# Router scale vectors stored in rows, router weight product behind the first output tile, routing in the order of the first gather

## The chip, the cores and the metric

The kernel runs on one core of a Trainium2 chip as one program. The metric is the device time of one execution in microseconds, the median of three timed runs. Beside them stands one profiled execution of the same program, from which every row below is taken.

## The reference, cut to what matters

The model takes one sequence of 512 tokens of width 1024 in f32. Four first layers (two short convolutions, a state space mixer, an RWKV mixer) are followed by two layers that each hold a token mixer and a hierarchical mixture of 32 experts. The change touches the step from the second kind of token mixer into its mixture of experts, in both layers:

```python
for l in range(DEPTH_2):
    mod = (c_act @ w_ada[l] + b_ada[l])[:, None, :]
    sh1, sc1, g1, sh2, sc2, g2 = jnp.split(mod, 6, axis=-1)
    h = rms_norm(x, norm1_g[l]) * (1 + sc1) + sh1
    x = x + g1 * token_mixer(h, ...)
    h = rms_norm(x, norm2_g[l]) * (1 + sc2) + sh2
    x = x + g2 * hierarchical_moe(h, router_group_w[l], router_group_b[l],
                                  router_expert_w[l], router_expert_b[l], w1[l], w3[l], w2[l])
```

The mixture picks for each token the best of 4 groups of experts and in it the two best of 8 experts, weighs them by a softmax, and adds the two experts' outputs (`silu(h @ w1) * (h @ w3)) @ w2`, with expert matrices of 1024x512, 1024x512 and 512x1024).

## The kernel before, in words

A tile scheduler lays the instructions of each engine in one order when the program is built; `self.behind(ins)` is a hint to it that what is issued inside stands behind the instruction `ins`. On the chip every engine then works through its list in that order, so an instruction that waits holds up all that stand behind it on its engine. SP issues the DMAs, also in order.

**The end of a token mixer.** `moe_before` (L2198) prepares the router while the mixer still runs. For the first of the two layers it stores four vectors of 1024 numbers, the gains `gs` and the shifts `mod` of both layers, into a DRAM scratch `d_gp` (L2205, L2206). In SBUF such a vector lies as 128 partitions by 8 columns, in DRAM as 8 rows of 128, so the store goes element by element. L2477 reads them back as `gp` in the layout that the gather of the experts needs. Then come the loads of the router's weights `wr` and bias `rb` (L2209, L2210), the product `gw` of weights and gains on VectorE (L2211), eight matmuls of `wr` with the shifts (L2214), and their sum with `rb` (L2215). The mixer's last matrix `w_out` is loaded in eight parts through the helper at L338, split into two halves of the f32 precision on ScalarE and VectorE (L315, L317), and multiplied at L423; `out_sink` adds each of the eight result tiles into the residual `xp`. In the second half of the tiles `moe_part` (L2222) also forms the router's logits from `gw`.

**Routing.** `route` is a generator in three parts. The first part (to L2302) finds group and experts of each token, forms the softmax weights `wts` (L2274 to L2281), ranks each token in its expert (`cs`, `rk`, `rx`, `r8`), and computes on GpSimd the slots `main0` of the tokens of the two static experts 0 and 1 (L2295 to L2302). The second part ranks all experts by their counts (`key`, `big`, `rank`, `ecap`, `nb`, L2306 on) and yields the list `eii` of experts in order of size. `moe_gather` (L2444) turns slots into selection matrices: GpSimd writes `Ra` and VectorE `R` for four blocks of tokens (L2454, L2455), and matmuls of `R` with the two halves of the hidden state (L2464) give the gathered tokens, which ScalarE scales into `xg` (L2468).

**The experts.** Expert weights come in loads of 1 MB (L2394) into 11 buffers, `raw`; an expert takes six (two of `w1`, two of `w3`, two of `w2`). Experts 0 and 1 are static, so 11 of their 12 loads are issued before routing is done. All others are loaded by the number read from `eii`. `moe_up` (L2401) multiplies by `w1` and `w3` (L2411), `moe_down` (L2423) by `w2` (L2438). Between routing and the first expert stands `overflow` (L2659, L2663), a loop for tokens beyond an expert's slots whose count is read from `eii`; its head and its end are points at which all engines wait for each other. In the profiled execution the loop has no pass.

```python
first = self.moe_gather(l, main, *GROUPS[0], gx)
next(first)
main = next(route)
self.fill(first, 99)
wts, over, eii = next(route)
...
    self.overflow(l, eii, over, wts)
...
    gs = self.moe_up(ws, gx[g], units)
```

## Time and profile before

| | |
|---|---|
| median of 3 timed runs | 3358.76 us (3357.37 to 3361.43) |
| profiled execution | 3351.78 us |
| its span, first to last instruction | 3350.0 us |
| granted TensorE clock, mean over the span | 0.921 |
| first four layers, then the modulation and mixer of layer 0 | 0 to about 1934 us |
| mixture of experts of layer 0 | about 1934 to 2490 us |
| mixer of layer 1 | about 2490 to 2790 us |
| mixture of experts of layer 1 | about 2790 to 3350 us |

The profile gives for each engine when it worked and, where it stood idle, what ended the idle time. PE is TensorE, DVE VectorE, ACT ScalarE, POOL GpSimd, SP the engine that issues the DMAs. A granted clock of 1.00 is TensorE's level of 2.4 GHz, 0.50 that of 1.2 GHz.

### The profile page before, as it was taken

The page shows a single profiled execution, that of the slowest core. Times are in us where ns is not written, and L with a number is a line of the kernel's source. Part 1 is how long each engine was busy: PE and PEld are TensorE (multiplying, and loading weights), DVE is VectorE, ACT ScalarE, POOL GpSimd, SP SyncE. Part 2 cuts the span into 40 slices and gives each one's busy share as a digit, 9 for nine tenths or more (in the row PEclk, how much of TensorE's full clock was granted, in tenths as well). Part 3 has the DMA queues.
Part 4 walks back from the last instruction along what each step waited for, and adds up shares of the span by engine and source line. Part 5 has one row for each costly group of instructions (what it writes and reads, how often), then busy time and mean ns, then how long its engine had stood idle before and what let it go on. Part 6 is the DMA issues. An engine that isn't in the chain of part 4 may idle for free. (4 is left out here: it accounts for less than half of the span.)

```text
span 3350.0 us, 57495 instructions
## 1 busy us (share of the span) xinstructions
PE 2979.4 (89%) x23218; PEld 2154.2 (64%) x23218; DVE 2016.2 (60%) x3911; ACT 1032.3 (31%) x1696; POOL 882.7 (26%) x738
## 2 busy tenths in 40 slices
PE   7999889988889898999789979989979996998997
PEld 5677768865557777777655756555647565655554
DVE  6754495467875778798847554534436845354443
ACT  3233324356533433222343421111125342111111
POOL 2911331125422456421205220100111423010000
PEclk9999899989889898999788979999989887999999
DMA  5453463314679545676340049999972003899998
GB/s 170 135 157 101 127 165 102 104 63 127 176 212 251 166 150 176 195 219 205 104 53 20 26 189 360 408 409 416 415 272 70 28 20 152 307 415 410 416 416 337
DMA packets 443070, 690.46 MB, mean 206 GB/s; under 512 B 68720, under 2 KB 354800, under 8 KB 408944
## 3 DMA queue, kind: packets, MB, share of 16 engines
q1 hardware_dynamic: 441648, 684.63, 58.9%
q8 instruction: 185, 3.03, 0.4%
q10 hardware_dynamic: 1152, 2.10, 0.2%
q14 instruction: 85, 0.70, 0.1%
HBM read 642.08 MB, written 46.94 MB: 206 GB/s over the span
## 5 line engine op out<-in xcount | busy, mean ns | idle before, releaser
L317 DVE TENSOR_TENSOR wl<-wr,wh 128x1024 fp32r<-128x1024 f32 (+2 forms) x275 | 327.8, 1194 | 213.6 <-ACT wh L315 110.4
L315 ACT ACTIVATE wh<-wr 128x1024 fp32r<-128x1024 f32 (+2 forms) x290 | 271.0, 939 | 532.6 <-PE pmm L423 177.6
L2411 PE MATMUL pmm<-raw,xg 128*32 128x128 f32 (+1 forms) x5120 | 351.4, 324 | 2.7 <-DMA raw<-in_w_dram 2.5
L2411 PEld LDWEIGHTS pmm<-raw,xg 128*32 128x32 f32 (+1 forms) x5120 | 228.2, 123 | 121.0 <-issue 48.8
L2558 POOL TENSOR_SCALAR Ra<-sp,cf 128x512 f32<-128x512 f32 x28 | 44.6, 1593 | 795.0 <-PE pst L2597 744.3
L423 PE MATMUL pmm<-H,wh 128*128 128x512 f32 x680 | 205.7, 412 | 12.2 <-ACT wh L315 8.2
L423 PE MATMUL pmm<-L,wh 128*128 128x512 f32 x680 | 203.1, 406 | 3.7 <-DVE L L317 2.2
L423 PE MATMUL pmm<-H,wl 128*128 128x512 f32 x680 | 202.3, 405 | 1.5 <-DVE wl L317 1.5
L2573 DVE SCALAR_TENSOR_TENSOR xp<-pst,mod,xp 128x512 f32<-128x512 f32 x196 | 143.0, 748 | 64.8 <-PE pst L2598 60.5
L2438 PE MATMUL pas<-raw,gT 128*32 128x256 f32 (+1 forms) x1472 | 171.1, 465 | 12.0 <-DVE gT L2432 9.8
L423 PEld LDWEIGHTS pmm<-H,wh 128*128 128x128 f32 x680 | 130.6, 197 | 45.0 <-ACT wh L315 9.9
L1561 DVE SCALAR_TENSOR_TENSOR war<-wa,cs,war 128x256 f32<-128x256 f32 x252 | 157.1, 640 | 3.5
L423 PEld LDWEIGHTS pmm<-L,wh 128*128 128x128 f32 x680 | 130.7, 194 | 37.0 <-DVE L L317 4.1
L423 PEld LDWEIGHTS pmm<-H,wl 128*128 128x128 f32 x680 | 131.4, 195 | 33.7 <-DVE wl L317 2.4
L2648 ACT COPY Y<-pas 32x256 f32<-32x256 f32 (+1 forms) x92 | 37.8, 411 | 298.9 <-DVE Y L2648 298.8
L2464 PE MATMUL pst<-R,hH 128*128 128x320 f32 (+4 forms) x448 | 92.7, 323 | 33.4 <-DVE R L2455 30.8
L2438 PEld LDWEIGHTS pas<-raw,gT 128*32 128x32 f32 (+1 forms) x1472 | 61.2, 122 | 93.8 <-issue 61.0
L2648 DVE COPY Y<-pas 32x256 f32<-32x256 f32 (+1 forms) x92 | 43.7, 475 | 128.7 <-PE pas L2438 120.2
L2418 DVE TENSOR_TENSOR g<-g,pmm 128x256 f32<-128x256 f32 (+1 forms) x56 | 20.3, 363 | 162.3 <-ACT g L2417 162.0
L2417 ACT ACTIVATE g<-pmm 128x256 f32<-128x256 f32 (+1 forms) x56 | 18.9, 338 | 294.0 <-PE pmm L2411 294.0
L2411 PE MATMUL pas<-raw,xg 128*32 128x128 f32 (+1 forms) x2048 | 97.8, 292 | 10.9 <-SPq L2518 6.8
L2464 PEld LDWEIGHTS pst<-R,hH 128*128 128x128 f32 x448 | 69.7, 202 | 56.7 <-DVE R L2455 35.6
(869 smaller groups left out, 6729.2 us busy)
## 6 DMA issues: line engine op xcount, KB each, us to landing
raw<-in_w_dram SPq DMA_DIRECT2D x384, 1024.0 KB, 12.4
wa<-in_w_ada_dram SPq DMA_DIRECT2D x48, 1024.0 KB, 5.9
wr<-in_conv_w_in_dram SPq DMA_DIRECT2D x64, 512.0 KB, 4.7
wr<-in_w_in_dram SPq DMA_DIRECT2D x34, 512.0 KB, 4.1
wr<-in_ple_gate_dram SPq DMA_DIRECT2D x16, 1024.0 KB, 5.5
wr<-in_rwkv_w_rkvz_dram SPq DMA_DIRECT2D x16, 1024.0 KB, 5.7
wr<-in_conv_w_out_dram SPq DMA_DIRECT2D x8, 1024.0 KB, 5.2
wr<-in_ssm_w_in_dram SPq DMA_DIRECT2D x8, 1024.0 KB, 6.5
```

What stands on the lines that cost most here:

```text
L315: self.nc.scalar.activation(h, x, AF.Copy)
L317: (eng or self.nc.vector).tensor_tensor(l, x, h.bitcast(FT), OP.subtract)
L423: nc.tensor.matmul(ps[i], ws[i][w][:, perm[k]], x[k], start=n == first[i], stop=n == last[i])
L1561: E.scalar_tensor_tensor(acc, w[:, k], cs[:, k:k + 1], acc, op0=OP.mult, op1=OP.add)
L2411: nc.tensor.matmul(p[c * n:c * n + n, w // 2 * W:w // 2 * W + W], x[:, j, o:o + n], ws[w][:, jj, c * W:c * W + W], start=j == 0, stop=j == 7)
L2417: nc.scalar.activation(g, p[:, 0:W], AF.Sigmoid)
L2418: nc.vector.tensor_tensor(g, g, p[:, 0:W], OP.mult)
L2438: nc.tensor.matmul(py[q * n:q * n + n, 0:W], gT[:, o:o + n], ws[4 + j // 2][:, j % 2, q * W:q * W + W], start=j == 0, stop=j == 3)
L2464: T.matmul(p[:, :n], (self.hH, self.hL)[i // 4][:, i % 4, j], R[:, i % 4, :n], start=i == 0, stop=i == 7)
L2558: G.tensor_scalar(a, P[0], s, None, op0=OP.is_equal)
L2573: self.done = self.nc.vector.scalar_tensor_tensor(self.xp[m], p, self.mod[l][:, 40 + m:41 + m], self.xp[m], op0=OP.mult, op1=OP.add).ins
L2648: (nc.scalar.copy if q % 2 else nc.vector.tensor_copy)(self.block[1][o:o + n, q * W:q * W + W], p[q * n:q * n + n])
```

## The change

Four things change; all other code stays.

1. `moe_before` no longer stores the four vectors element by element. PE transposes each into 8 rows of 128, ScalarE copies the 8x512 tile to SBUF, and one DMA stores its rows into `d_gp`.
2. The product `gw`, the eight matmuls with `wr` and the sum with `rb` move into `moe_weights`, which is issued behind the first output tile (`first_sink`, m = 0). The loads of `wr` and `rb` stay where they were.
3. In `route`, `main0` is computed on VectorE in five instructions instead of on GpSimd in eight; the copy `sh` of the slots falls away where its offset is 0; the softmax weights are formed behind `main0`; and the second part is issued behind the last `R` of the first gather.
4. In `moe`, `moe_up` of the experts 0 and 1 and the twelfth load of the static experts are issued ahead of `overflow`.

```diff
--- before.py
+++ after.py
@@ -2179,12 +2179,18 @@
 
 
         def out_sink(m, p):
-            V.scalar_tensor_tensor(self.xp[m], p, self.mod[l][:, 16 + m:17 + m], self.xp[m], op0=OP.mult, op1=OP.add)
+            return V.scalar_tensor_tensor(self.xp[m], p, self.mod[l][:, 16 + m:17 + m], self.xp[m], op0=OP.mult, op1=OP.add).ins
+
+        def first_sink(m, p):
+            done = out_sink(m, p)
+            if m == 0:
+                with self.behind(done):
+                    self.moe_weights(l)
 
         def last_sink(m, p):
             out_sink(m, p)
             self.moe_part(l, m)
-        for h, sink in enumerate((out_sink, last_sink)):
+        for h, sink in enumerate((first_sink, last_sink)):
             o = order[h * 4:h * 4 + 4]
             self.dense(([z["H", k] for k in o], [z["L", k] for k in o]), A["w_out"][l][h * 512:h * 512 + 512], range(0, D, 256),
                        sink, kt=4, perm=[k - h * 4 for k in o])
@@ -2201,17 +2207,26 @@
         if self.d_gp is None:
 
             self.d_gp = d = self.dr.tile([2, 2, 8, 128], FT, name="d_gp")
+            p = self.pt("tp", bufs=2)
             for i in range(2):
-                nc.sync.dma_start(d[i, 0].rearrange("k p -> p k"), self.gs[i][:, 8:16])
-                nc.sync.dma_start(d[i, 1].rearrange("k p -> p k"), self.mod[i][:, 24:32])
-        wr, self.gw, self.rb = (self.c2.tile([128] + sh, FT, name=f"{n}{l}", tag=n, bufs=1)
-                                for n, sh in (("wr", [8, 36]), ("gw", [8, 36]), ("rb", [36])))
-        nc.sync.dma_start(wr, self.A["w_router"][l].rearrange("(k p) n -> p k n", p=128))
+                for j, t in enumerate((self.gs[i][:, 8:16], self.mod[i][:, 24:32])):
+                    o = (2 * i + j) * 128
+                    nc.tensor.transpose(p[0:8, o:o + 128], t, self.ident)
+            t = self.wt("rows")
+            nc.scalar.activation(t[0:8], p[0:8], AF.Copy)
+            nc.sync.dma_start(d.rearrange("i j k p -> k (i j) p"), t[0:8].rearrange("k (n p) -> k n p", n=4))
+        self.wr, self.gw, self.rb = (self.c2.tile([128] + sh, FT, name=f"{n}{l}", tag=n, bufs=1)
+                                     for n, sh in (("wr", [8, 36]), ("gw", [8, 36]), ("rb", [36])))
+        nc.sync.dma_start(self.wr, self.A["w_router"][l].rearrange("(k p) n -> p k n", p=128))
         nc.sync.dma_start(self.rb, self.A["rb"][l])
-        nc.vector.tensor_tensor(self.gw, wr, self.gs[l][:, 8:16, None].to_broadcast([128, 8, 36]), OP.mult)
+
+    def moe_weights(self, l):
+
+        nc = self.nc
+        nc.vector.tensor_tensor(self.gw, self.wr, self.gs[l][:, 8:16, None].to_broadcast([128, 8, 36]), OP.mult)
         p = self.pt("st", bufs=2)
         for k in range(KT):
-            nc.tensor.matmul(p[:, 0:36], self.mod[l][:, 24 + k:25 + k].to_broadcast([128, 128]), wr[:, k], start=k == 0, stop=k == KT - 1)
+            nc.tensor.matmul(p[:, 0:36], self.mod[l][:, 24 + k:25 + k].to_broadcast([128, 128]), self.wr[:, k], start=k == 0, stop=k == KT - 1)
         nc.vector.tensor_tensor(self.rb, self.rb, p[:, 0:36], OP.add)
         self.ps2, self.pl, self.st2 = self.pt("st", bufs=2), self.pt("st", bufs=2), []
 
@@ -2248,9 +2263,6 @@
             V.tensor_tensor(c, c, bc(ix, n), OP.is_equal)
         goh = t("goh", (4, 4))
         first_max(g, 4, col(0), goh, "g")
-        ge = t("ge", (4, 4))
-        V.tensor_tensor(ge, g, bc(col(0), 4), OP.subtract)
-        ACT.activation(ge, ge, AF.Exp)
         em = t("em", (4, 32))
         e4 = em.rearrange("p j (g e) -> p j g e", g=4)
         pen = t("pen", (4, 4))
@@ -2270,15 +2282,6 @@
         bf = both.rearrange("p j e -> p (j e)")
         T.matmul(pc[:, 0:128], self.ones, bf, start=True, stop=True)
         T.matmul(pr[:, 0:128], self.cm("tri"), bf, start=True, stop=True)
-        wts = mo.tile([128, 2, 4], FT, name=f"wts{l}", tag="wts", bufs=1)
-        V.tensor_tensor(col(4), col(3), col(2), OP.subtract)
-        ACT.activation(col(4), col(4), AF.Exp)
-        V.tensor_reduce(col(1), ge, axis=AX.X, op=OP.add)
-        V.reciprocal(col(1), col(1))
-        V.tensor_scalar(col(5), col(4), 1.0, None, op0=OP.add)
-        V.reciprocal(col(5), col(5))
-        V.tensor_tensor(wts[:, 0], col(5), col(1), OP.mult)
-        V.tensor_tensor(wts[:, 1], wts[:, 0], col(4), OP.mult)
         cs, rk = t("cs", (4, 32)), t("rk", (4, 32))
         pc4 = pc[:, 0:128].rearrange("p (j e) -> p j e", j=4)
         V.tensor_copy(cs[:, 0], pc4[:, 0])
@@ -2292,15 +2295,24 @@
         V.tensor_reduce(r8, rx, axis=AX.X, op=OP.add)
 
         main0, main1 = (mo.tile([128, 8], FT, name=f"main{i}{l}", tag=f"main{i}", bufs=1) for i in range(2))
-        G.tensor_scalar(main0, r8, 1.0, None, op0=OP.add)
-        G.tensor_tensor(main0, main0, oh8[:, :, 0], OP.mult)
-        G.tensor_scalar(main1, r8, 1.0 + PLACE[1], None, op0=OP.add)
-        G.tensor_tensor(main1, main1, oh8[:, :, 1], OP.mult)
-        G.tensor_tensor(main0, main0, main1, OP.add)
-        G.tensor_scalar(main1, r8, float(CAPS[0]), None, op0=OP.is_lt)
-        G.tensor_tensor(main0, main0, main1, OP.mult)
-        G.tensor_scalar(main0, main0, -1.0, None, op0=OP.add)
+        V.scalar_tensor_tensor(main0, r8, 1.0, oh8[:, :, 0], op0=OP.add, op1=OP.mult)
+        V.scalar_tensor_tensor(main1, r8, 1.0 + PLACE[1], oh8[:, :, 1], op0=OP.add, op1=OP.mult)
+        V.tensor_tensor(main0, main0, main1, OP.add)
+        V.scalar_tensor_tensor(main0, r8, float(CAPS[0]), main0, op0=OP.is_lt, op1=OP.mult)
+        V.tensor_scalar(main0, main0, -1.0, None, op0=OP.add)
         yield main0.rearrange("p (q j) -> p q j", q=2)
+        ge = t("ge", (4, 4))
+        V.tensor_tensor(ge, g, bc(col(0), 4), OP.subtract)
+        ACT.activation(ge, ge, AF.Exp)
+        wts = mo.tile([128, 2, 4], FT, name=f"wts{l}", tag="wts", bufs=1)
+        V.tensor_tensor(col(4), col(3), col(2), OP.subtract)
+        ACT.activation(col(4), col(4), AF.Exp)
+        V.tensor_reduce(col(1), ge, axis=AX.X, op=OP.add)
+        V.reciprocal(col(1), col(1))
+        V.tensor_scalar(col(5), col(4), 1.0, None, op0=OP.add)
+        V.reciprocal(col(5), col(5))
+        V.tensor_tensor(wts[:, 0], col(5), col(1), OP.mult)
+        V.tensor_tensor(wts[:, 1], wts[:, 0], col(4), OP.mult)
 
         key, rank, big = t("key", (32,)), t("rank", (32,)), t("big", (32, 32))
         V.scalar_tensor_tensor(key, cnt, 32.0, self.cm("ekey"), op0=OP.mult, op1=OP.add)
@@ -2444,16 +2456,18 @@
         nc = self.nc
         V, G, T, ACT = nc.vector, nc.gpsimd, nc.tensor, nc.scalar
         s, X = self.tl(f"sh{N}", (2, 4)), f"{N}" if N < 320 else ""
-        if isinstance(base, int):
-            (V if base else G).tensor_scalar(s, place, float(-base), None, op0=OP.add)
+        if isinstance(base, int) and base == 0:
+            s = place
+        elif isinstance(base, int):
+            V.tensor_scalar(s, place, float(-base), None, op0=OP.add)
         else:
             V.tensor_scalar(s, place, base, None, op0=OP.subtract)
         R = self.tl("R" + X, (4, N), FR, bufs)
         for j in range(4):
             a = self.tl("Ra" + X, (N if X else S,), bufs=bufs)
             G.tensor_scalar(a[:, :n], self.cm("slot")[:, 0:n], s[:, 0, j:j + 1], None, op0=OP.is_equal)
-            V.scalar_tensor_tensor(R[:, j, :n], self.cm("slot")[:, 0:n], s[:, 1, j:j + 1], a[:, :n],
-                                   op0=OP.is_equal, op1=OP.add)
+            self.done = V.scalar_tensor_tensor(R[:, j, :n], self.cm("slot")[:, 0:n], s[:, 1, j:j + 1], a[:, :n],
+                                               op0=OP.is_equal, op1=OP.add).ins
         yield
         x = self.tl("xg" + X, (8, N), bufs=bufs)
         out.append(x)
@@ -2468,6 +2482,12 @@
                 ACT.activation(x[:, j, :n], p[:, :n], AF.Identity, scale=gain[:, j:j + 1], bias=shift[:, j:j + 1])
             yield
 
+    @staticmethod
+    def units(r, g):
+
+        o = PLACE[r] - GROUPS[g][0]
+        return [(o + u, min(CAPS[r] - u, 64)) for u in range(0, CAPS[r], 64)]
+
     def moe(self, l, begin):
         ro = ExitStack()
         self.ro = ro.enter_context(self.tc.tile_pool(name="ro", bufs=1, reuse_waits="tile"))
@@ -2478,6 +2498,7 @@
         loads = {0: self.moe_loads(l, 0), 1: self.moe_loads(l, 1, self.NRAW - 6)}
         if begin:
             self.moe_before(l)
+            self.moe_weights(l)
             for k in range(KT):
                 self.moe_part(l, k)
         rstd = self.rms_rows(self.ps2, D)
@@ -2504,8 +2525,15 @@
         gx = []
         first = self.moe_gather(l, main, *GROUPS[0], gx)
         next(first)
-        main = next(route)
+        with self.behind(self.done):
+            main = next(route)
         self.fill(first, 99)
+
+        begun = {}
+        for r in range(NSTATIC):
+            self.fill(loads[r][1], 6)
+            units = self.units(r, 0)
+            begun[r] = self.moe_up(loads[r][0], gx[0], units)
         wts, over, eii = next(route)
         ro.close()
         with self.tc.tile_pool(name="ov", bufs=1, reuse_waits="tile") as self.ov:
@@ -2525,9 +2553,8 @@
                 fill = self.moe_gather(l, main, *GROUPS[g + 1], gx) if g + 1 < len(GROUPS) else None
                 if not fill:
                     self.last_selections(l, spread)
-            o = PLACE[r] - GROUPS[g][0]
-            units = [(o + u, min(CAPS[r] - u, 64)) for u in range(0, CAPS[r], 64)]
-            gs = self.moe_up(ws, gx[g], units)
+            units = self.units(r, g)
+            gs = begun.pop(r) if r in begun else self.moe_up(ws, gx[g], units)
             self.fill(fill, 5 if g < 1 else 3)
             if prev:
                 self.moe_store(blocks, *prev)
```

How the order changes on SP, at the end of the mixer of layer 0 (`w_in` is the mixer's first matrix, `w_out` its last). Before:

```order
L338 DMA wr_14833<-in_w_in_dram 128x8x128
L2205 DMA d_gp<-gs_13250 128x8x1
L2206 DMA d_gp<-mod_78 128x8x1
L2205 DMA d_gp<-gs_13253 128x8x1
L2206 DMA d_gp<-mod_79 128x8x1
L2209 DMA wr_15245<-in_w_router_dram 128x8x36
L2210 DMA rb_15247<-in_rb_dram 128x36
L2477 DMA gp<-d_gp 128x4x8
L338 DMA wr_15493<-in_w_out_dram 128x4x256
```

With the change:

```order
L338 DMA wr_14833<-in_w_in_dram 128x8x128
L2220 DMA wr_15249<-in_w_router_dram 128x8x36
L2221 DMA rb_15251<-in_rb_dram 128x36
L338 DMA wr_15484<-in_w_out_dram 128x4x256
L338 DMA wr_15486<-in_w_out_dram 128x4x256
L338 DMA wr_15537<-in_w_out_dram 128x4x256
L338 DMA wr_15575<-in_w_out_dram 128x4x256
L2217 DMA d_gp<-rows_15246 8x4x128
L2497 DMA gp<-d_gp 128x4x8
L338 DMA wr_15649<-in_w_out_dram 128x4x256
```

The router's loads now follow the mixer's loads directly; the store of the rows and the load of `gp` stand behind the fourth of the eight loads of `w_out`.

On VectorE, in the routing of layer 0, from the ranks `rx` to the selection matrices `R`. Before:

```order
L2306 SCALAR_TENSOR_TENSOR key_16070<-cs_16033,cf_13391 128x32
L2291 TENSOR_TENSOR rx_16041<-oh_16004,rk_16034 128x256
L2309 TENSOR_TENSOR big_16072<-key_16070 128x1024
L2292 TENSOR_REDUCE r_16042<-rx_16041 128x8
L2310 TENSOR_REDUCE rank_16071<-big_16072 128x32
L2315 TENSOR_TENSOR rx_16041<-oh_16004,rank_16071 128x256
L2329 TENSOR_TENSOR big_16072<-rank_16071,cf_13391 128x1024
```

With the change:

```order
L2294 TENSOR_TENSOR rx_16033<-oh_16005,rk_16026 128x256
L2295 TENSOR_REDUCE r_16034<-rx_16033 128x8
L2298 SCALAR_TENSOR_TENSOR main_16037<-r_16034,oh_16005 128x8
L2299 SCALAR_TENSOR_TENSOR main_16038<-r_16034,oh_16005 128x8
L2300 TENSOR_TENSOR main_16037<-main_16037,main_16038 128x8
L2301 SCALAR_TENSOR_TENSOR main_16037<-r_16034,main_16037 128x8
L2302 TENSOR_SCALAR main_16037<-main_16037 128x8
L2469 SCALAR_TENSOR_TENSOR R_16045<-cf_13391,main_16037,Ra_16046 128x192
L2469 SCALAR_TENSOR_TENSOR R_16045<-cf_13391,main_16037,Ra_16049 128x192
```

The reduce that gives `r8` no longer stands behind the wide `big`, the five instructions of `main0` follow it, and the four `R` come ahead of the whole second part.

On PE, at the loop `overflow` of layer 0 (`pst` are the gather's results, `pas` and `pmm` at L2411 those of `moe_up`). Before:

```order
L2464 MATMUL pst_16170<-R_16057,hH_15917 128x192 x4
L2464 MATMUL pst_16170<-R_16057,hL_15918 128x192 x4
L2659 TENSOR_LOAD eii_16097
L2663 COMPARE_AND_BRANCH
...
L2663 UNCONDITIONAL_BRANCH
L2411 MATMUL pas_16514<-raw_15879,xg_16099 64x256 x8
L2411 MATMUL pmm_16515<-raw_15879,xg_16099 32x128 x16
```

With the change:

```order
L2478 MATMUL pst_16170<-R_16045,hH_15921 128x192 x4
L2478 MATMUL pst_16170<-R_16045,hL_15922 128x192 x4
L2423 MATMUL pas_16180<-raw_15885,xg_16099 64x256 x4
...
L2423 MATMUL pas_16288<-raw_15901,xg_16099 64x256 x8
L2423 MATMUL pmm_16289<-raw_15901,xg_16099 32x128 x16
L2686 TENSOR_LOAD eii_16097
L2690 COMPARE_AND_BRANCH
```

Both up-projections, partly woven into the gather's matmuls, now stand ahead of PE's read of `eii` and of the loop's head; behind the loop the second group's gather comes first.

## Rows read from the trace of the kernel before

**Rows 1.** The page's first part: busy us of an engine, share of the span, instructions.

```profile
PE 2979.4 (89%) x23218; PEld 2154.2 (64%) x23218; DVE 2016.2 (60%) x3911; ACT 1032.3 (31%) x1696; POOL 882.7 (26%) x738
```

**Rows 2.** Windows, layer 0: stretch, length, busy PE PEld DVE ACT POOL, clock, DMA share, GB/s.

```profile
1735.00:1745.00 10.00, 0.00 (x0) 0.00 (x0) 0.00 (x0) 0.00 (x0) 0.00 (x0) 0.72 1.65 11
1751.00:1760.00 9.00, 9.00 (x30) 4.93 (x31) 5.77 (x10) 2.33 (x6) 1.94 (x2) 0.50 0.19 58
```

**Rows 3.** Waits, 1726 to 1760: who waited for what, total us, times, longest.

```profile
DVE gw L2211 <- DMA wr<-in_w_router_dram: 18.7, 1, 18.7
PE pas L2016 <- DVE mq L2018: 16.2, 1, 16.2
```

**Rows 4.** DMAs issued from 1726 to 1765: packets, and KB each with us to landing.

```profile
DMA packets 7443, 1.29 MB, mean 33 GB/s; under 512 B 5904, under 2 KB 7440, under 8 KB 7440
...
wr<-in_w_router_dram SPq DMA_DIRECT2D x1, 144.0 KB, 18.8
```

**Rows 5.** PE's timeline, same two places in both layers: start, us, instruction [idle before].

```profile
1727.16 0.60 PE L2009 MATMUL ptp<-ident,my 128*8 128x128 f32 x4
...
1915.24 0.53 PE L2222 MATMUL pst<-gw,xp 128*128 128x36 f32 x4
...
2602.37 0.60 PE L2009 MATMUL ptp<-ident,my 128*8 128x128 f32 x4
...
2772.11 0.64 PE L2222 MATMUL pst<-gw,xp 128*128 128x36 f32 x5
```

**Rows 6.** Waits of DVE, 2602 to 2605 (layer 1).

```profile
DVE gw L2211 <- DMA wr<-in_w_router_dram: 0.8, 1, 0.8
```

**Rows 7.** Waits of SP, 1726 to 1915.

```profile
SPq L338 <- DVE wl L317: 154.7, 8, 54.7
```

**Rows 8.** DVE's timeline in the routing of layer 0.

```profile
1956.10 0.16 DVE L2280 TENSOR_TENSOR wts<-sm 128x4 f32<-128x4 f32 x1
...
1958.94 1.22 DVE L2309 TENSOR_TENSOR big<-key 128x1024 f32<-128x1024 f32 x1
1960.08 0.41 DVE L2292 TENSOR_REDUCE r<-rx 128x8 f32<-128x256 f32 x1
```

**Rows 9.** POOL's timeline in the routing of layer 0.

```profile
1963.68 1.18 POOL L2448 TENSOR_SCALAR sh<-main 128x8 f32<-128x8 f32 x1
1964.95 3.09 POOL L2454 TENSOR_SCALAR Ra<-cf,sh 128x192 f32<-128x192 f32 x4
```

**Rows 10.** PE's timeline, first gather of layer 0 (last wait, last matmuls).

```profile
1969.19 0.93 PE L2464 MATMUL pst<-R,hH 128*128 128x192 f32 x3 [1.23 <-DVE R L2455]
...
1978.27 0.61 PE L2464 MATMUL pst<-R,hL 128*128 128x192 f32 x4
```

**Rows 11.** PE's timeline, up-projections of experts 0 and 1 in layer 0.

```profile
1982.31 1.11 PE L2411 MATMUL pas<-raw,xg 128*64 128x256 f32 x3 [3.43 <-SPq L2663]
...
1988.91 1.95 PE L2411 MATMUL pas<-raw,xg 128*64 128x256 f32 x16
...
1997.58 0.80 PE L2464 MATMUL pst<-R,hH 128*128 128x288 f32 x4
...
2018.25 0.80 PE L2464 MATMUL pst<-R,hH 128*128 128x288 f32 x4
```

**Rows 12.** PE's timeline at the same places of layer 1.

```profile
2842.46 3.38 PE L2411 MATMUL pas<-raw,xg 128*64 128x256 f32 x16 [6.77 <-SPq L2518]
...
2876.14 0.80 PE L2464 MATMUL pst<-R,hH 128*128 128x288 f32 x4
```

**Rows 13.** PE's branches of the loop, both layers: ns min/median/max, first and last start.

```profile
L2663 PEldq COMPARE_BRANCH  x6: 70/185/3942, 1980.4 to 2842.2; - x6
```

**Rows 14.** Windows in the mixtures of experts, columns as in rows 2.

```profile
1980.00:2030.00 50.00, 46.96 (x591) 33.11 (x595) 15.07 (x43) 12.08 (x20) 6.42 (x5) 0.93 0.51 176
...
2960.00:3240.00 280.00, 255.20 (x2879) 158.45 (x2879) 121.33 (x244) 37.25 (x79) 28.46 (x24) 0.98 1.02 414
```

**Rows 15.** SP's timeline behind the loop of layer 0.

```profile
1989.05 8.99 SPq L2394 DMA_DIRECT2D raw<-in_w_dram  x4
```

## The prediction

> **What bounds the kernel now.** I read the page's busy shares first. PE works 89% of the span [rows 1], so time is lost only where PE stands still or runs at the low clock, or where PE waits for weights. The windows show the first such place that the change touches. From 1735 to 1745 us, at the end of layer 0's mixer, every engine shows 0.00 busy, while the DMA engines are taken up (the share printed is 1.65) and move 11 GB/s; after it the granted clock is 0.50, the 1.2 GHz level, for another 9 us [rows 2]. The waits name the reason: VectorE's `gw` at L2211 waits 18.7 us for `wr`, and PE waits 16.2 us for `mq`, which stands behind `gw` on VectorE [rows 3]. The list of DMAs says why `wr` is late: 5904 of that stretch's 7443 packets are under 512 B, and `wr`, 144 KB, takes 18.8 us to land behind them [rows 4]. Those are `d_gp`'s four element-wise stores. In layer 1, which has no such stores, the same `gw` waits 0.8 us [rows 6].
>
> The second place is the start of each mixture of experts. PE waits for the selection matrices until 1969.19, runs the gather to 1978.9 (1978.27 and 0.61) [rows 10], stands 3.43 us at the loop and starts the first up-projection at 1982.31 [rows 11]; in layer 1 it stands 6.77 us [rows 12]. From 1980 to 2030 the DMAs move 176 GB/s, against 414 GB/s later on, when their share is 1.02 [rows 14]. So the experts are bound by the loads once these run, and the start costs because the loads begin late there: buffers come free only as the first up-projections read them, and SP issues the first load behind the loop at 1989.05 [rows 15].
>
> **Part 1 and 2: rows in place of elements, the product later.** Without the small stores, and with `gw` no longer ahead of `mq`, the stall has no cause left. Its price is read from layer 1, which runs the same code without it. From the L2009 matmuls to the first L2222, layer 0 takes 1915.24 - 1727.16 = 188.08 us, layer 1 2772.11 - 2602.37 = 169.74 us [rows 5]: 18.3 us more, which is the stall plus the slow clock behind it, less what layer 0 makes up later. I take -18.3. Bounds: -16.2 is PE's idle time alone, and -19.2 VectorE's wait with 0.5 for `gw` itself [rows 3].
>
> What is added: four transposes on PE, which I take from the four L2009 matmuls of the same 128-column form, 0.60 us together [rows 5], and a copy and a store that nobody near waits for. +0.6, bounds 0 and +1.2. On SP the store and the load of `gp` move behind the fourth load of `w_out`. Behind them are queued the last four of `w_out` and all expert loads, but SP waits 154.7 us in eight waits for VectorE's splits there, up to 54.7 in one [rows 7]; the store and load take the place of such a wait. The eight matmuls with `wr` and the two VectorE instructions only move: 0. Layer 1 loses its 0.8 us wait for `wr` [rows 6]: -0.8. Sum of these parts: -18.5.
>
> **Part 3: routing.** VectorE's `big` (1.22 us, begun at 1958.94) stands ahead of `r8`'s reduce, which ends at 1960.49 [rows 8]. `Ra` starts on POOL at 1964.95 [rows 9], 4.46 us later; in between lie eight small POOL instructions and `sh` (1.18 us [rows 9]). With the change the reduce moves up by some 1.1 us, and five dependent VectorE instructions of 128x8 take their place, which I set at 0.2 us each by the 0.16 us of a 128x4 one [rows 8]. So `Ra` starts at 1960.49 - 1.1 + 1.0 = 1960.4. Four `Ra` of 0.77 us (3.09 in all [rows 9]) end at 1963.5, and the last `R` near 1964.1: PE's gather goes on 5.1 us earlier than at 1969.19. POOL's instructions behind it (the second part's) are later than `Ra` in both orders, and the softmax weights are not needed before the experts' outputs.
>
> **Part 4: up-projections ahead of the loop.** The gather takes 9.7 us from there (to 1973.8). Three of the four 1 MB loads of an up-projection take 1997.58 - 1988.91 = 8.67 us at clock 1.00 [rows 11], so two whole ones take 23.1 us and PE is done near 1997.0. All operands are there: the first eleven loads are issued before the routing ends. Then comes the loop. It adds a wait: every engine, SP with the loads of expert 2 and all later ones among them, is let go only when PE, ScalarE and VectorE have finished the up-projections. With 1 us for their last results and the rest of the 3.43 us gap seen before, that is near 2000.6 in place of 1982.3.
>
> What it gives on PE: of the 20.67 us from 1997.58 to 2018.25 [rows 11] the second up-projection is 11.6, so 9.1 us of other work (gather pieces, spreads) then remain: PE is at 2009.7 where it was at 2018.25, 8.5 us ahead. Of this some 2.3 us go again, if the clock falls at the loop as it did before (the first up-projection took 1997.58 - 1982.31 = 15.3 us for 11.6): 6.2 us ahead. On the loads: seven buffers are free at the release, so 7 MB go out at once. Allowing 1.5 us to their first bytes (my choice), at 414 GB/s (27.9 us to 2030) and with the 1 MB ahead of the loop, 12.6 MB are moved by 2030, where it was 176 GB/s times 50 us = 8.8 MB [rows 14]; 3.8 MB are 9.2 us. The loads set the end, PE is close behind them, and I take -8 in layer 0.
>
> In layer 1 PE restarts at 2842.46 after 6.77 us idle, 3.34 us more than in layer 0 [rows 12], with one branch of 3.94 us on PE [rows 13]; SP is not held by it. If that branch stays where it is, PE comes out 3.3 us less far ahead, but it was as late before, so I take -7. The Trainium skill, page "Runtime: NRT & Kernel Launch", section "Instruction fetch mechanics", says that a taken branch to a target outside the two fetched pages waits for a fetch, an instruction-fetch stall. That fits the one long branch, but by that rule the jump over the unused loop body would pay in both layers, and layer 0's gap shows no such time; were it paid in both, this part would be worth 3.3 us less in layer 0. Bounds of parts 3 and 4, for a layer: +11.5, if the loads behind the loop begin at 2000.6 and not 1989.05 [rows 15] and none of it is regained; and -12.2, if PE's 5.1 us, its 3.4 us gap and its 3.7 us of slow clock all come off. My value lies near the second, because what the loads can do with free buffers is a row of this trace (414 GB/s), while nothing in it shows free buffers left unfilled.
>
> **Sum.** -18.5 - 8 - 7 = -33.5 us. The profiled execution took 3351.8 us, which gives 3318.3; the median of the timed runs is 7.0 us above it, and I apply the same difference there: 3358.8 - 33.5 = 3325.3, forecast 3325.
>
> **Rivals.**
> A, only the stall goes: the loads that now start at 2000.6, not 1989.05, give back what the early up-projections win. For it: PE and the loads are both near full after 2030, so there is little to catch up with. Against it: 7 free buffers at once. -18.5 alone: 3340.
> B, the upper bounds: -18.5 - 24.4 = -43: 3316. For it: layer 1's branch and both clocks may recover behind the loads. Against it: a new idle gap of PE at the loop is certain.
> C, slower: the release at the loop waits for PE and also for its code, so that SP is let go at 2003.9 (2000.6 and 3.3), 14.9 us after 1989.05, and the loads then run at their old mean, so that all of it is lost: 2 x 14.9 - 18.5 = +11: 3370. It decides if the loads' first bytes come later than about 2020 (old equal of a full stream: 2030 less 8.8 MB at 414, 2008.7, plus 2.4 for the early MB, plus half of 18.5). That is 20 us behind my release; the trace gives no such time.
> D, the change doesn't remove the stall, since something else in the `mq` chain is late: -15 alone, 3344. The layer 1 rows speak against it.
>
> **How the numbers follow.** Forecast 0.55 (its own range, with the bounds of the stall and -5 to -10 a layer, 3318 to 3332); A 0.20, B 0.15, D 0.05, C 0.03, and 0.02 for no change, where A and D come together. About 0.2% (6.7 us) can be told from no change. Faster then has 0.95, same 0.02, slower 0.03. The range takes in the forecast's own, A with 2 us beyond it for the spread of the timed runs, and most of B: 3310 to 3342. D, C and no change lie outside it, with the rest of B.
>
> **What would show it.** Right: no idle stretch near 1735 to 1750; the wait at the new `gw` line under 1 us; the first logit matmul (L2222 before) some 18 us earlier; last `R` about 4 us after `r8`; PE idle once near the end of both up-projections and not ahead of them; several 1 MB loads issued within 2 us of the release, with 400 GB/s behind it. Wrong: a wait of SP at the row store or at `gp` with `w_out` late behind it; a new stall on VectorE at `gw` or the bias sum; a second gap of the loads, 5 us or more, between the burst and the steady stream, which would turn the forecast into A.

## The result and the profile after

| | before | with the change |
|---|---|---|
| median, first set | 3358.41 us (4 runs) | 3321.64 us (4 runs, 3318.32 to 3335.82) |
| ratio, 95% interval | | 0.9897 (0.9877 to 0.9918) |
| median, second set | 3355.87 us (17 runs, 3343.01 to 3372.73) | 3325.06 us (6 runs, 3321.47 to 3335.28) |
| ratio, 95% interval | | 0.9907 (0.9878 to 0.9936) |
| profiled execution | 3351.78 us | 3323.11 us |

The change makes the kernel some 1% faster: 34.6 us by the first ratio (27.5 to 41.3), 31.2 by the second (21.5 to 40.9). The forecast was 3325.

Where it went is read first in the windows, at the place of the stall (columns: stretch, length, busy time of PE, PEld, DVE, ACT, POOL, granted clock, DMA share, GB/s):

```profile
1725.00:1735.00 10.00, 10.00 (x65) 5.71 (x64) 7.61 (x15) 5.11 (x11) 2.84 (x3) 1.00 0.32 86
1735.00:1745.00 10.00, 9.86 (x122) 5.24 (x120) 5.44 (x7) 2.54 (x6) 4.38 (x4) 1.00 0.01 2
```

Where all engines stood at 0.00 [rows 2], PE now works 9.86 of 10 us at clock 1.00, and the DMA engines are free. The waits of VectorE from 1723 to 1760 us no longer name `gw`, as [rows 3] did; the longest belong to the chain from `mq` on:

```profile
DVE mq L2018 <- PE pas L2016: 5.0, 3, 2.6
DVE hd L1815 <- ACT hd L1812: 3.2, 3, 2.1
```

The row store and the load of `gp` are in SP's timeline behind the fourth load of `w_out`, 1.5 us apart, and nobody waits for them:

```profile
1840.03 0.36 SPq L2217 DMA_DIRECT2D d_gp<-rows  x1
1841.54 0.38 SPq L2497 DMA_DIRECT2D gp<-d_gp  x1
```

In the kernel before, the four stores went out from 1726.8 on, right ahead of the router's loads, and took 16 to 18 us each to land (KB each, us to landing):

```profile
d_gp<-gs SPq DMA_DIRECT2D x2, 4.0 KB, 16.3
d_gp<-mod SPq DMA_DIRECT2D x2, 4.0 KB, 17.6
```

Part 1 thus changes two things at once: the form of the store, and its place, which is now some 110 us later. That `gp`, which reads what the store wrote, goes out 1.5 us behind it shows the row store to be short; whether element-wise stores at the late place would have done no harm either, no run shows.

The same two marks of PE as in [rows 5] (L2237 is the new line of the first logit matmul), with the first matmul of the gather, the end of the up-projections and the restart behind the loop in layer 0 and, last row, the restart in layer 1:

```profile
1722.87 0.60 PE L2009 MATMUL ptp<-ident,my 128*8 128x128 f32 x4
...
1889.87 0.53 PE L2237 MATMUL pst<-gw,xp 128*128 128x36 f32 x4
...
1936.67 2.65 PE L2478 MATMUL pst<-R,hH 128*128 128x192 f32 x7 [4.05 <-DVE R L2469]
...
1974.26 1.08 PE L2423 MATMUL pmm<-raw,xg 128*32 128x128 f32 x32
1979.40 1.33 PE L2478 MATMUL pst<-R,hH 128*128 128x288 f32 x4 [4.07 <-issue]
...
2833.65 1.33 PE L2478 MATMUL pst<-R,hH 128*128 128x288 f32 x4 [4.96 <-issue]
```

The mixer of layer 0 takes 167.0 us between its marks, for 188.1. PE waits 4.05 us for the selection matrices and then runs through the gather and both up-projections; its idle time at the loop now stands behind them, 4.07 and 4.96 us. VectorE's timeline shows the new order of the routing:

```profile
1933.82 0.42 DVE L2295 TENSOR_REDUCE r<-rx 128x8 f32<-128x256 f32 x1
1934.28 0.17 DVE L2298 SCALAR_TENSOR_TENSOR main<-r,oh 128x8 f32<-128x8 f32 x1
...
1934.97 0.17 DVE L2302 TENSOR_SCALAR main<-main 128x8 f32<-128x8 f32 x1
1936.05 0.57 DVE L2469 SCALAR_TENSOR_TENSOR R<-cf,main,Ra 128x192 fp32r<-128x192 f32 x1 [0.91 <-POOL Ra L2468]
...
1938.26 0.42 DVE L2469 SCALAR_TENSOR_TENSOR R<-cf,main,Ra 128x192 fp32r<-128x192 f32 x1 [0.17 <-POOL Ra L2468]
```

Five instructions of 0.17 us, 0.9 us in all, then `Ra` and `R`: the last `R` ends 4.4 us after `r8` (1934.24). The windows at the loop show what the loads do with it; the first of them is the stretch that answers to 1980 to 2030 in [rows 14], laid at the same distance from the first logit matmul:

```profile
1954.66:2004.66 50.00, 45.72 (x602) 34.26 (x601) 18.28 (x54) 13.59 (x23) 7.33 (x6) 0.93 0.51 196
1980.00:1990.00 10.00, 10.00 (x68) 10.00 (x67) 3.58 (x6) 1.99 (x4) 1.56 (x1) 0.78 1.00 419
1990.00:2000.00 10.00, 9.79 (x80) 6.31 (x82) 7.11 (x28) 5.21 (x9) 5.16 (x4) 1.00 0.69 281
2000.00:2010.00 10.00, 10.00 (x171) 7.62 (x163) 5.36 (x11) 4.35 (x7) 0.00 (x0) 1.00 0.89 350
```

The burst behind the loop is there (419 GB/s). Behind it lies a second gap, which makes the 281 and 350 GB/s of the last two rows: from 1996 to 2002 us the loads move 87 GB/s, 0.5 MB in place of some 2.5. The only wait of SP from 1978 to 2000 (second row here) names what it stands for, the down-projection of expert 0 (L2450):

```profile
1996.00:2002.00 6.00, 6.00 (x110) 3.52 (x110) 2.73 (x10) 1.54 (x4) 0.26 (x1) 1.00 0.30 87
```

```profile
SPq L2406 <- PE pmm L2450: 18.5, 1, 18.5
```

PE runs its first 5 us behind the loop at the low clock (0.78 over the 10 us from 1980). In the 50 us the loads move 9.8 MB, for 8.8 before. PE begins the down-projection of expert 0, first before and then with the change, at

```profile
2023.04 3.65 PE L2438 MATMUL pas<-raw,gT 128*64 128x512 f32 x16
```

```profile
1994.96 3.65 PE L2450 MATMUL pas<-raw,gT 128*64 128x512 f32 x16
```

that is 107.8 and 105.1 us after the first logit matmul: 2.7 us earlier, less than the 4.4 us by which the gather begins earlier (next section).

### The profile page after: what moved, and what is told of

Read it like the earlier page. It is cut to its first block, busy times and chain, and to the rows that moved or that the text cites. A ratio compares the mean times of both kernels' runs of the same rounds, so it can differ in the third digit from the quotient of the medians.

```text
span 3321.3 us, 57502 instructions
## 1 busy us (share of the span) xinstructions
PE 2982.6 (90%) x23222; PEld 2155.7 (65%) x23222; DVE 2013.6 (61%) x3921; ACT 1032.3 (31%) x1696; POOL 872.9 (26%) x720
## 2 busy tenths in 40 slices
DMA packets 438950, 690.46 MB, mean 208 GB/s; under 512 B 64568, under 2 KB 350680, under 8 KB 404824
## 5 line engine op out<-in xcount | busy, mean ns | idle before, releaser
L2450 PE MATMUL pas<-raw,gT 128*32 128x256 f32 (+1 forms) x1472 | 164.7, 449 | 13.8 <-DVE gT L2444 11.8
L2450 PEld LDWEIGHTS pas<-raw,gT 128*32 128x32 f32 (+1 forms) x1472 | 59.4, 119 | 96.6 <-issue 57.5
L2086 DVE SCALAR_TENSOR_TENSOR cc<-cu,vec,cc 128x512 f32<-128x512 f32 x120 | 102.2, 852 | 1.4
```

Source lines behind the costliest of these rows:

```text
L2086: V.scalar_tensor_tensor(acc, t[:, j:j + S], self.v2(f"dw{i}{j}", l), acc, op0=OP.mult, op1=OP.add)
L2450: nc.tensor.matmul(py[q * n:q * n + n, 0:W], gT[:, o:o + n], ws[4 + j // 2][:, j % 2, q * W:q * W + W], start=j == 0, stop=j == 3)
```

## The experiments

Executions of one kernel differ by up to 38 us here (before: 3342 to 3380 in one set). The ratios below are against the kernel before in the same set; they come from three sets, each on another chip, in which that kernel has medians of 3358.61, 3355.87 (the second set of the table above) and 3350.76 us. Parts 1 and 2, parts 1 to 3, part 4 alone and the early loads belong to the one with 3358.61, for which there is no time of the unaltered change; so where one of these four is compared with the change, the chip is a rival that no run excludes. Each kernel is also read by stretches of its profile, between marks that all of them have: the first L2009 of a mixer, its first logit matmul, the first gather matmul, and the next mixer's L2009 or the end. Each row is one profiled execution. All in us:

| profile | mixer 0 | routing 0 | experts 0 | mixer 1 | routing 1 | experts 1 |
|---|---|---|---|---|---|---|
| before | 188.0 | 51.2 | 636.0 | 169.7 | 51.2 | 526.7 |
| before, second profile | 189.2 | 51.1 | 635.5 | 172.4 | 51.1 | 527.1 |
| part 4 alone | 192.8 | 51.2 | 635.5 | 168.8 | 51.2 | 533.0 |
| parts 1 and 2 | 171.5 | 51.2 | 634.4 | 185.4 | 51.2 | 528.5 |
| part 1 alone | 163.3 | 51.4 | 635.5 | 173.0 | 51.2 | 531.7 |
| part 1 alone, again | 165.1 | 51.2 | 632.9 | 176.1 | 51.2 | 531.2 |
| part 2 alone | 172.3 | 51.2 | 634.4 | 171.8 | 51.2 | 530.8 |
| parts 1 to 3 | 173.9 | 46.8 | 639.9 | 169.3 | 47.0 | 535.9 |
| the change | 167.0 | 46.8 | 636.1 | 170.4 | 46.8 | 531.3 |
| the change, again | 167.0 | 46.8 | 635.3 | 170.1 | 47.1 | 535.5 |
| parts 1, 3 and 4 | 169.7 | 46.8 | 636.9 | 171.9 | 45.4 | 534.2 |
| change, third expert's loads early | 170.0 | 46.8 | 636.4 | 176.2 | 47.0 | 530.5 |
| change, one up-projection early | 169.9 | 46.8 | 631.7 | 170.1 | 46.8 | 531.7 |
| parts 1, 3 and 4, one up-projection | 168.2 | 46.8 | 633.2 | 169.0 | 46.6 | 530.0 |

**Parts 1 and 2 alone.** The routing, the up-projections and the twelfth load as before. Here and below, a diff is against the changed kernel; the routing's own lines, put back as they were, are left out:

```diff
-        with self.behind(self.done):
-            main = next(route)
+        main = next(route)
...
-        for r in range(NSTATIC):
-            self.fill(loads[r][1], 6)
-            units = self.units(r, 0)
-            begun[r] = self.moe_up(loads[r][0], gx[0], units)
```

> Parts 1 and 2 of the change alone (vectors stored in rows, weight product behind the first output tile), routing and experts as before. Theory of the stall: the 18.7 us wait of gw is gone and nothing takes its place, so 18 to 21 us off the 3358.4 of before: 3337 to 3340. Rival (something else in that chain is late, or the whole gain of the change sits in the experts): above 3350.

Measured: 3346.76 us, ratio 0.9961 (0.9945 to 0.9977), 13 us faster. The stall is gone (171.5 for 188 to 193), so the theory holds for its stretch; the total falls short of the 18 to 21 us expected. Its profiled execution (3352.01 us) shows one place: layer 1's mixer, with as many matmuls as elsewhere, took 185.4 us. The windows of that stretch, here and in the kernel with part 4 alone:

```profile
2584.80:2770.20 185.40, 174.91 (x1470) 112.20 (x1469) 110.66 (x249) 68.88 (x142) 65.27 (x63) 0.79 0.09 28
2674.80:2684.80 10.00, 10.00 (x80) 6.28 (x79) 2.48 (x10) 1.32 (x4) 1.90 (x3) 0.50 0.01 2
```

```profile
2599.40:2768.20 168.80, 158.33 (x1470) 104.65 (x1469) 109.95 (x249) 66.25 (x140) 64.46 (x63) 0.85 0.10 30
```

PE is idle 10.5 us in both; the first has a mean clock of 0.79, the second 0.85, and that makes 16.6 us. Why the clock fell more here, and whether it did in the other executions, no run shows.

**Part 1 alone, twice.** The product `gw` stays at its old place, parts 3 and 4 are undone as above.

```diff
         nc.sync.dma_start(self.rb, self.A["rb"][l])
+        self.moe_weights(l)
...
-            if m == 0:
-                with self.behind(done):
-                    self.moe_weights(l)
```

> Part 1 alone: rows in place of elements, the weight product at its old place. If the element-wise stores make the router's weights late, gw's wait falls from 18.7 us to about the 0.8 us of layer 1 and the mixer of layer 0 (first L2009 to first logit matmul) takes 170 us for 188. If the stores are not the cause, gw still waits over 10 us.

> Part 1 alone once more, for a second profile and more times. If the rows alone do all that ends the stall: 18 to 21 us below before in the mixer of layer 0 and in the median (3336 to 3340). The first five times (median 3320.8) would then have been the clock's luck. If they were not, 3320 again, as fast as the whole change.

Measured: 3320.76 us (0.9884, 0.9848 to 0.9919) and 3322.32 us (0.9908, 0.9875 to 0.9942). The mixer of layer 0 falls to 163.3 and 165.1 us. `gw`, still ahead of `mq`, waits 1.6 us:

```profile
DVE gw L2224 <- DMA wr<-in_w_router_dram: 1.6, 1, 1.6
```

The 144 KB of `wr` land after 4.5 us, for 18.8 [rows 4]:

```profile
wr<-in_w_router_dram SPq DMA_DIRECT2D x1, 144.0 KB, 4.5
```

The element-wise stores ahead of the router's loads are the cause, and part 1 alone ends the stall. In total it is as fast as the whole change (0.9897 and 0.9907), so the totals show no gain of parts 2 to 4 beyond it; the 18 to 21 us that I expected of it were too few. It is also clearly faster than parts 1 and 2 together (0.9961, another set), though the later product costs nothing in the run without part 2 below. What makes these totals differ isn't shown.

**Part 2 alone.** The element-wise stores are back, the product comes later, parts 3 and 4 are undone as above.

```diff
             for i in range(2):
-                for j, t in enumerate((self.gs[i][:, 8:16], self.mod[i][:, 24:32])):
...
+                nc.sync.dma_start(d[i, 0].rearrange("k p -> p k"), self.gs[i][:, 8:16])
+                nc.sync.dma_start(d[i, 1].rearrange("k p -> p k"), self.mod[i][:, 24:32])
```

> Part 2 alone: the element-wise stores stay, the weight product comes behind the first output tile. The weights still land some 19 us late, but nothing waits for them: the mixer of layer 0 takes 170 us for 188 too, so either part alone would do. Rival: the stores also hold SP's queue and the first loads of w_out, and part of the stall stays (175 us or more).

Measured: 3336.80 us, 0.9937 (0.9915 to 0.9958); mixer of layer 0 172.3 us. The router's load still lands after 17.5 us, and `gw` runs right behind the first output tile with no wait:

```profile
wr<-in_w_router_dram SPq DMA_DIRECT2D x1, 144.0 KB, 17.5
```

```profile
1871.09 0.75 DVE L2182 SCALAR_TENSOR_TENSOR xp<-pmm,mod,xp 128x512 f32<-128x512 f32 x1
1871.76 0.45 DVE L2221 TENSOR_TENSOR gw<-wr,gs 128x288 f32<-128x288 f32 x1
```

So either part alone ends the stall, and the two gains don't add.

**The change without part 4.**

```diff
         begun = {}
-        for r in range(NSTATIC):
-            self.fill(loads[r][1], 6)
-            units = self.units(r, 0)
-            begun[r] = self.moe_up(loads[r][0], gx[0], units)
```

> The change without part 4: the up-projections of experts 0 and 1 stand behind the loop again. By the prediction, part 4 is worth some 3 us a layer beyond the 5 us of the routing, so 3321.6 + 6 = 3328. Rival, from the bytes moved since the first gather (after 200 us 74.2 MB with the change, 75.4 before): part 4 gives back some 3 us a layer by holding the loads, so 3321.6 - 6 = 3316.

Measured: 3335.51 us, 0.9929 (0.9911 to 0.9948). Neither sum fits: by the ratios it is 7 to 11 us slower than the change, though the intervals overlap and the sets are not the same. The bytes that the rival rests on take in the routing, which the change shortens; counted from the first gather, the change and the kernel before both move 64.0 MB in 200 us (320 GB/s). The waits of PE in layer 0 show a cost that neither case had (1945 to 1975 us), with the read of `eii` for the loop by SP:

```profile
PE pas L2423 <- SPq L2542: 13.3, 1, 13.3
PE pst L2478 <- DVE R L2469: 4.1, 1, 4.1
```

```profile
L2682 SPq TENSOR_LOAD <-eii x1: 270/270/270, 1966.9 to 1966.9; - x1
```

The read comes 66.6 us after the first logit matmul (1900.3); before it came at 1979.7, 64.5 us after 1915.2. The gather begins 4.4 us earlier, but the second part of the routing, held behind the last `R`, ends 2 us later, and PE now waits 13.3 us at the loop, where it waited 3.4 [rows 11]. In the table the 4.4 us come back as 639.9 and 535.9. By the stretches part 3 without part 4 wins nothing. The medians alone would say otherwise, for parts 1 and 2 took 3346.76 us in the same set, 11 us more; but in the two profiles that difference lies in layer 1's mixer (185.4 and 169.3 us), which part 3 doesn't touch.

**Part 4 alone on the kernel before.** Stores, product and routing as before; against the kernel before, the edit is (with the lines behind the loop that take the finished products)

```diff
         self.fill(first, 99)
+        begun = {}
+        for r in range(NSTATIC):
+            self.fill(loads[r][1], 6)
+            units = self.units(r, 0)
+            begun[r] = self.moe_up(loads[r][0], gx[0], units)
```

> Part 4 alone on the kernel before. By the prediction 3 us a layer are won: 3358.4 - 6 = 3352. By the rival the loads held behind the loop cost 3 us a layer: 3358.4 + 6 = 3364.

Measured: 3354.18 us, 0.9989 (0.9972 to 1.0006): neither. Its stretches show no gain either: experts 635.5 and 533.0. SP is ready at the loop and waits 15 us for VectorE, the last to come, and PE goes on at 2005.61:

```profile
SPq L2682 <- DVEq L2678: 15.0, 1, 15.0
```

```profile
2005.61 1.09 PE L2472 MATMUL pst<-R,hH 128*128 128x288 f32 x3 [2.13 <-DVEq L2682]
```

So here the list is ready before the up-projections are, and they would cover the late list of part 3. That parts 3 and 4 need each other is argued from these waits; that the two together win more than either by itself, the totals don't show.

**The third expert's loads ahead of the loop.**

```diff
         wts, over, eii = next(route)
+        r = ORDER[NSTATIC]
+        e = nc.values_load(eii[0:1, r:r + 1], engines=[mybir.EngineType.SP], min_val=0, max_val=31)
+        loads[r] = self.moe_loads(l, e)
```

> The change, and in addition the six loads of the third expert are issued ahead of the loop, as buffers come free from the up-projections. If the start of the loads sets the end of a layer, 6 MB that move in the idle 1950 to 1980 us are worth up to 6/0.414 = 14 us a layer, less what PE cannot follow: 3321.6 - 10 to - 25, 3297 to 3312. If PE sets the end behind the loop, 3318 to 3322.

Measured: 3334.58 us, 0.9942 (0.9923 to 0.9962, in another set than the change): no gain, if not a loss. The windows and PE's wait behind the loop:

```profile
1965.00:1975.00 10.00, 10.00 (x192) 6.95 (x194) 1.42 (x4) 0.66 (x2) 0.00 (x0) 1.00 0.85 307
...
1985.00:1995.00 10.00, 8.41 (x45) 8.41 (x46) 1.34 (x3) 1.51 (x3) 1.56 (x1) 0.61 0.33 108
1995.00:2005.00 10.00, 9.79 (x69) 7.78 (x69) 8.65 (x30) 5.09 (x9) 5.16 (x4) 1.00 0.01 2
```

```profile
PE pst L2478 <- SPq L2693: 8.1, 1, 8.1
```

The loads did run early (307 GB/s in the stretch that was empty), but then the buffers were full: 2 GB/s from 1995 to 2005, because PE, held 8.1 us at the loop while SP issued them, had gathers and spreads to do before it freed another. In this run PE's work sets the pace at the start of a layer, not the loads.

**One up-projection ahead of the loop, the other behind it.**

```diff
-        for r in range(NSTATIC):
+        for r in range(1):
```

> The change with only expert 0's up-projection ahead of the loop; expert 1's stands behind it. If the loads of the later experts start too late behind the loop, SP is let go some 12 us earlier and the loads run on: 3 to 6 us a layer, 6 to 12 us below the unaltered change. If PE's own work at the start of a layer sets the pace (as the extra loads of the run before suggest: more loads early, no gain), the time is that of the unaltered change within 4 us.

Measured: 3328.90 us, 0.9914 (0.9882 to 0.9947), against 3325.06 (0.9907) for the change in the same set: within 4 us, as the second case has it. The stretches lean the other way (631.7 and 531.7 for about 635.7 and 533.4), with a shorter gap at the loop behind which the clock stays at 1.00:

```profile
1964.67 0.81 PE L2478 MATMUL pst<-R,hH 128*128 128x288 f32 x4 [2.44 <-DVEq L2690]
```

**The change once more,** unaltered.

> The changed kernel once more, unaltered, beside the others. Theory of the pieces: between the marks of its profile (first logit matmul, first gather, end of each layer) the change wins 21 us in the stall and 3 to 4 in both mixtures together, so its median should lie near 3358.6 - 24 = 3334 over more executions. Rival: the first four executions (median 3321.6) were typical and the mixtures win 7 us each as predicted: 3319 to 3325.

Measured: 3325.06 us. The rival stands, at its upper end: the first executions were typical (the kernel before was some 3 us faster in this set). The sum of my pieces is smaller by 7 to 11 us than the two ratios give; it lies within the second ratio's interval and below the first's.

**The kernel before once more,** unaltered.

> The kernel before, unaltered, for a second profile of it. The first profiled execution was 7 us below the median of the timed ones. If executions differ by the clock granted in the mixers (as between profiles of other kernels here: 163 to 185 us for the same work at a mean clock of 0.87 to 0.79), the extra lies in those stretches, at about 51.2 us from first logit matmul to first gather and 16 us of idle PE in the stall as before. Rival: the extra lies in the mixtures of experts (above 636 and 527 us).

Measured: 3348.89 us, 0.9993 (0.9969 to 1.0017), beside 3350.76 for the same kernel in that set. Its profile again was below the other sets' medians, with stretches within 3 us of the first; the rows of `gw` (16.5 us) and `mq` (14.0 us) are there again. The expectation that it would show where the medians lie higher was not met.

**The change without part 2, and that with one up-projection early.** The edits are those shown at part 1 alone and at the single up-projection:

```diff
         nc.sync.dma_start(self.rb, self.A["rb"][l])
+        self.moe_weights(l)
...
-        for r in range(NSTATIC):
+        for r in range(1):
```

> The change without part 2: the weight product stands where it stood before, everything else is new. If the rows are what ends the stall and the later product only costs order (163 us with the rows alone for the mixer of layer 0, 171.5 with both), this is 4 to 8 us below the change, 3317 to 3321. If both parts are equal within the clock's spread, 3323 to 3327.

> As the run before, and only expert 0's up-projection ahead of the loop. From the last profile of that kind (631.7 us for 635.7 from first gather to the next mixer in layer 0, 531.7 for 533.4 in layer 1) 2 to 6 us below the run before. If that was the clock's luck, within 3 us of it.

Measured: 3326.36 us (0.9917, 0.9887 to 0.9946) and 3315.22 us (0.9882, 0.9847 to 0.9918). The first equals the change, so beside the rows the later product is worth nothing. The second is the lowest median of all, 0.9882 for the change's 0.9897 and 0.9907, but the intervals overlap. It is 11 us below the run before, more than either case had. That it beats the change is likely from its stretches (633.2 and 530.0 us for the experts), not shown. Its profiled execution, 3301.66, also had the shortest untouched first part (below).

## Why the prediction was right, and where its steps were not

The time was forecast within 4 us, and the direction and the place of the largest term were right. That the sum came so near is luck in part: one term was too small, one far too large, and 7 to 11 us of the gain lie in no stretch that the change touches. Term by term, from the table:

**The stall: right in mechanism, undersized.** I took -18.3 and +0.6. Mixer 0 takes 188.0, 189.2 and 192.8 us with the stall (mean 190.0), and 167.0 to 173.9 in the five profiles with parts 1 to 3 (mean 169.6): -20.4. In these means PE's idle time falls from 25.8 to 11.3 us, and its busy time, for nearly the same matmuls, by the other 5.9 us, at a mean clock of 0.81 with the stall and 0.86 without. Layer 1, which I took as the measure, is itself no clean one: 168.8 to 185.4 us. That the rows and the later product would each do it alone I did not say; both runs show it. The prediction also read all 5904 small packets of [rows 4] as the stores; four vectors of 1024 elements make 4096, and the pages count 68720 small packets before and 64568 after.

**SP and the added work: right.** The row store and `gp` stand behind the fourth load and nobody waits for them; the four transposes take 0.6 us (1838.68 to 1839.28), as set. **Layer 1's `gw` wait** (-0.8) is lost in the spread of that mixer.

**The routing: right.** `Ra` was set to begin 4.6 us earlier and the gather to go on 5.1 us earlier; the stretch shrinks by 4.4 us in layer 0 in every kernel with part 3, and by 4.1 to 5.8 us in layer 1. The five instructions were set at 0.2 us each; they take 0.17 us and begin 0.1 to 0.2 us apart.

**The up-projections ahead of the loop: oversized.** The step that failed is the credit for the loads, "seven buffers are free at the release, so 7 MB go out at once", run on at 414 GB/s to 12.6 MB. The trace shows the 7 MB go out and then a gap of some 5 us, the length that the prediction had named as the sign of rival A: 9.8 MB in place of 12.6. Some 2 MB of the difference are the gap; the rest fits a later start, with PE done with both up-projections 85.5 us after the first logit matmul (1975.34) where the prediction had 81.8 (1997.0). The next buffer is freed by expert 0's down-projection, which stands behind the second gather and the transposes of `main` and `wts`; the run with the early loads shows that more loads do not help. PE shows the low clock behind the loop as forecast (the 2.3 us set for it are not what the prediction's own row gives, 15.3 - 11.6 = 3.7), but it is 2.7 us ahead at that down-projection and not 6.2. The table gives the experts, with the earlier gather counted in, 636.1 - 634.8 - 4.4 = -3.1 us in layer 0 and 533.7 - 529.3 - 4.4 = 0.0 in layer 1 (means of three profiles with parts 3 and 4 and six without either): -3 for the -15 of the sum, with rows of one kind that differ by 1.6 to 5.0 us. By the rows of layer 1 nothing was won there at all. Rival A, that only the stall goes, is nearly what the stretches show, and part 1 alone, as fast as the change, says the same.

**So the total fits better than its terms.** The stretches sum to about -20.4 - 3.1 - 0.8 (mixer 1, 170.25 for 171.05) = -24; the ratios give -31 and -35. Between the two profiled executions, -28.7, the stretches make -24.4 and the untouched first part -4.3. Some 7 to 11 us of the medians are left that no stretch shows. The first 1720 us, which the change doesn't touch, differ by more than that between profiles (below). Whether the change moves the clock there or in the mixers on average, or the sets drew well, stays open.

The long branch of layer 1 is there after as before: 3.5 us on PE at the loop's end, with a gap of 4.96 us for 4.07 in layer 0, whose longest branch there is 0.34 us. The rule of the Trainium skill, page "Runtime: NRT & Kernel Launch", section "Instruction fetch mechanics", is that a taken branch whose target is outside the two fetched pages waits for a fetch. The prediction took from it that both layers would pay, but the rule speaks only of targets outside those pages, and where they lie no run shows: the trace fits the rule in layer 1, and layer 0 speaks neither for it nor against it.

## What to carry to other kernels

A small store with scattered elements can hold up the loads issued behind it, here four of 4 KB each for some 14 us: transpose on PE and store rows, and look for the instruction that needs the delayed load and for what stands behind it on its engine. Work brought ahead of a point at which all engines wait holds the loads behind it too; before counting free buffers as bandwidth, ask which instruction frees the next ones. And an earlier first half can make the second half late: without part 4 the gather came 4.4 us sooner and the list that ended the wait at the loop 2 us later.

## What the runs showed of the hardware

The granted clock differs between executions of the same matmuls. Without the stall a mixer takes 163 to 185 us, in part by the clock: the two rows above, with 1470 matmuls each, show 0.79 and 0.85 at the same idle time, and beside the slower one stands a window with PE busy 10.00 of 10 us at 0.50, the 1.2 GHz level. The untouched first part, up to layer 0's L2009, took from 1706.1 to 1735.9 us over the fourteen profiles. Its extremes:

```profile
0.00:1706.00 1706.00, 1525.89 (x8974) 1209.01 (x8975) 1194.73 (x2137) 652.11 (x960) 591.88 (x472) 0.93 0.52 154
```

```profile
0.00:1735.80 1735.80, 1543.40 (x8974) 1221.36 (x8975) 1197.79 (x2137) 652.45 (x960) 589.26 (x472) 0.92 0.51 152
```

With the same 8974 matmuls, PE is busy 17.5 us longer and idle 12.3 us longer. One profile of each kernel therefore can't tell 10 us apart here; the marks of a stretch can where it repeats, as the routing's 51.2 and 46.8 us show. They repeat within 0.5 us but for one row of layer 1 (45.4), at mean clocks from 0.77 to 0.86: PE is busy there for only some 33 us, and the rest of the stretch is waits.
